# A two-block transformer on one core: first norm by a power operation, row scales moved out of two later norms, and five smaller moves

## The chip, the cores and the metric

The kernel runs on one core of one Trainium2 chip. The metric is device time in microseconds (us), from runs of the whole program. The core has a matrix engine (TensorE, PE in the profile, with its weight loads as PEld), a vector engine (VectorE, DVE), an activation engine (ScalarE, ACT), a general engine (GpSimd, POOL) and a queue engine that starts transfers (SyncE, SP). Matrix products write to the eight banks of PSUM; the other data is in SBUF.

## The reference

512 tokens of width 1024 go through two blocks, all in float32.

```
# first block
h = rmsnorm(x, norm_mix);  p = h @ w_in
y_ret  = retention(q, k, v, g of p; rotary sines and cosines of the positions)
y_rwkv = rwkv7(shifted p)          # gated delta-rule scan over time, group norm, bonus, gate
x = x + concat(y_ret, y_rwkv) @ w_out
x = x + cross_attention(rmsnorm(x, norm_xattn), rmsnorm(mem, norm_mem))   # 4 heads of 256, 256 memory rows
x = x + square(relu(rmsnorm(x, norm_mlp) @ w_up)) @ w_down                # 4096 wide
x = rmsnorm(x, norm_final)
# second block
h = rmsnorm(x); z = h @ w_in_2     # attention with axial rope, gated MLP with spatial mixing, merge gates
x = rmsnorm(x + merge(...) @ w_out_2)
```

A norm is `y = x * rsqrt(mean(x*x) + 1e-6) * gain`: one factor for each row (token) and one for each column.

## The kernel before

Tokens lie in four blocks of 128 rows. Every large product is made of three passes: each operand is split into a high part (a cast to fp32r, on ACT) and a low part (the rest, by a subtraction), and `mm3` adds high x high, high x low and low x high. Weights come as 512 KB units over SP's queue into three buffers, are split on ACT (L291, `wh`) and on DVE or POOL (L292, `wl`), and are used in order.

All matrix instructions keep the order in which the code writes them (`Ordered`). That order comes from generators: `streams` (L614) advances the main chain of products by one step, of some four matmuls, and then each side chain whose delay (`yield n`: n steps) or flag (`yield "name"`) has come. The other engines and the queues are ordered by the planner of the tile framework (`schedule_with_timeline_sim`), from its own estimate of durations: it puts an instruction on its engine when, by that estimate, its inputs are there and the engine is free, also ahead of earlier code. Each engine then works strictly in the order that was planned. What is changed lies here:

- `first` (L438): the first norm. The gain row is loaded to all 128 partitions; ACT squares four blocks; DVE makes `rsqrt` (L349, eleven small instructions) for two blocks at a time; blocks 0 and 1 are scaled on DVE, 2 and 3 on POOL and ACT; `turn` transposes eight 128x128 pieces for each block on PE, and splits them. Then the first product, 48 matmuls of 256 columns, follows.
- `trig` (L640): the angles' range reduction on POOL, some 60 instructions, and at its end two Sin activations on ACT (L685). The tables are used in the keys of the retention, much later.
- `products`, `invert`, `solve` (from L1521): RWKV's chunks. `invert` inverts 32x32 triangles on POOL, row by row; then two copies on ACT (L1586), transfers to DRAM and back (L1587 to L1595), and after 33 steps `solve` on PE reads the result. It is done twice, for two halves of the heads.
- `final_rw` (L818): for each of four pairs of heads transposes, an ACT instruction with weight and bias (L830), a POOL addition of `bv` (L831), a product with the gate (L836) and a split.
- `ret` (L750): the retention; `finish` transposes nine steps after its group norm.
- `run` (L428): one set of PSUM pools for the mixer (`mm`, `tp`, `cs`, `ch`, two banks each), and after it another (`mm` four, `tp`, `ch` two).
- `x1` (L975): the product with w_out in two halves of columns (`quad`), added to x (`add_x`, L936); `add_half` squares and multiplies by the gain on POOL (L955); `norm_end` makes the row's factor from the sums by `norm_scale`, multiplies (L970), and eight steps later transposes and splits. Then `tile_half` takes the first three Q tiles on the first 256 tokens and then on the rest. The second norm, for the MLP, is made in the same way after the product with w_o.
- `head`, `softmax` (L1051 to L1056): cross attention's scores with the scale 1/16.
- `heads` in `second` (L1174): rope in the second block.

Of the kernel before, what the change touches and what calls it, by code (L numbers as in the profile page):

```python
# [16 lines left out]
P = 128  # L17
# [65 lines left out]
def pack(inputs):  # L83
# [93 lines left out]
    for name, key in (("w0", "rwkv_w0"), ("a0", "rwkv_a0"), ("k_k", "rwkv_k_k"), ("k_a", "rwkv_k_a"), ("r_k", "rwkv_r_k"),  # L177
# [15 lines left out]
        "pv": pv,  # L193
        "rows": np.ascontiguousarray(rows),
# [34 lines left out]
class Kern:  # L229
# [34 lines left out]
    def psum(self, tag, shape=(P, 512)):  # L264
        return self.ps.tile(list(shape), F32, tag=tag, bufs=self.banks[tag], name=self.nm(tag))
# [162 lines left out]
    def run(self):  # L428
        nc, A, tc = self.nc, self.A, self.tc
        self.banks = {"mm": 2, "tp": 2, "cs": 2, "ch": 2}  # L430
        with tc.tile_pool(name="mx", bufs=1) as self.mp, tc.tile_pool(name="px", bufs=1, space=bass.MemoryType.PSUM) as self.ps:
            self.mix()
        self.banks = {"mm": 4, "tp": 2, "ch": 2}
        self.nh = 4
        with tc.tile_pool(name="m2", bufs=1) as self.mp, tc.tile_pool(name="p2", bufs=1, space=bass.MemoryType.PSUM) as self.ps:
            self.streams(self.rest())

    def first(self):  # L438
# [12 lines left out]
        g = self.gain("norm_mix", 6)  # L451
# [9 lines left out]
        v = [self.small(2) for _ in range(2)]  # L461
        rs = {}
        junk = self.slab(10, [P, 1024])

        def square(b):
            SC.activation(junk, xb[b], AF.Square, accum_out=v[b // 2][:, b % 2:b % 2 + 1])

        def chain(i):
            V.tensor_scalar(v[i], v[i], 1.0 / D, 1e-6, op0=ALU.mult, op1=ALU.add)
            r = self.rsqrt(v[i], 2, V=V)  # L470
            rs[2 * i], rs[2 * i + 1] = r[:, 0:1], r[:, 1:2]

        def scale(b):
            for h in range(2):
                c = slice(h * 512, h * 512 + 512)
                if b < 2:
                    V.scalar_tensor_tensor(xg[b][:, c], xb[b][:, c], rs[b], g[:, c], op0=ALU.mult, op1=ALU.mult)
                else:
                    SC.activation(xg[b][:, c], xg[b][:, c], AF.Copy, scale=rs[b])

        turn = lambda b: self.transp(xg[b], b, hh, V, SC, ("tp", "ch")[b % 2])
        for b in range(NB):
            square(b)
        for b in (2, 3):
            G.tensor_tensor(xg[b], xb[b], g, op=ALU.mult)
        chain(0)
        scale(0)
        scale(1)
        chain(1)
        turn(0)  # L490
        self.pump(0, 0, SC, G)
        turn(1)
        scale(2)
        scale(3)
        turn(2)
        turn(3)
        h, l = self.spl.pop(0)
        self.u = 1
        ps = self.psum("mm")
        for off in (0, 256):  # L500
            for k in range(KT):
                ah, al = h1[k]
                self.mm3(ps[:, off:off + 256], (h[:, k * 128:k * 128 + 128], l[:, k * 128:k * 128 + 128]),
                         (ah[:, off:off + 256], al[:, off:off + 256]), k == 0, k == KT - 1)
        derived(V)
# [134 lines left out]
    def trig(self):  # L640
# [45 lines left out]
        return  # L686
        yield
# [62 lines left out]
    def ret(self):  # L750
# [21 lines left out]
        def finish(n, y):  # L772
# [3 lines left out]
            yield 9  # L776
# [41 lines left out]
    def final_rw(self, hf, sl, s):  # L818
# [3 lines left out]
        for j in range(2):  # L822
# [7 lines left out]
            SC.activation(t, tr.rearrange("p c t -> p (c t)"), AF.Identity, bias=self.pv("rw_b", p), scale=self.pv("rw_w", p))  # L830
            G.tensor_tensor(t, t, self.bv[:, p], op=ALU.add)  # L831
# [108 lines left out]
    def add_half(self, st, b, j, ps, scale=None):  # L940
# [8 lines left out]
        self.flags.discard(f"norm {b}")  # L949
        ss, st[b][1] = st[b][0], self.tmp((P, 1024), "t4", 2)  # L950
        for i in range(4):
# [3 lines left out]
            nc.gpsimd.tensor_tensor(st[b][1][:, c], x[:, c], st["g"][:, c], op=ALU.mult)  # L955

# [7 lines left out]
    def norm_end(self, st, b, dst, rs=None, wait=None):  # L964

        ss, xg = st[b]
# [733 lines left out]
```

## Time and profile before

| | us |
|---|---|
| median of 3 runs | 1317.17 (1317.08 to 1317.53) |
| profiled execution | 1317.52 |
| its span, first to last instruction | 1315.7 |
| PE busy | 1244.0 (95%), 6972 matmuls |
| PEld, DVE, ACT, POOL busy | 1036.2, 708.0, 507.0, 472.7 |
| mean granted TensorE clock, share of full | 0.981 |

Times of events are counted from the start of the span. An engine's busy time is the sum over its instructions; "idle before" with a releaser says what ended an engine's wait. [...]

### The profile page before, as it was taken

What the parts mean: (1) busy time and instruction counts of PE and PEld (TensorE: products, weight loads), DVE (VectorE), ACT (ScalarE), POOL (GpSimd) and SP (SyncE); (2) the same over time, 40 slices, a digit from 0 to 9 for tenths busy, and PEclk for the clock granted to TensorE, in tenths of its full rate; (3) what the DMA queues carried; (4) which work ended last, traced back from release to release, by engine and by line L of the source; (5) the groups of instructions that cost most, each with busy time, mean ns of one, the idle gap of its engine ahead of it and who ended that gap; (6) DMA issues with size and microseconds to landing.
All of it is one profiled execution on the core that took longest, in us unless ns stands there. A gap on an engine that the chain in (4) does not pass through costs nothing.

```text
span 1315.7 us, 18199 instructions
## 1 busy us (share of the span) xinstructions
PE 1244.0 (95%) x6972; PEld 1036.2 (79%) x6972; DVE 708.0 (54%) x1493; ACT 507.0 (39%) x899; POOL 472.7 (36%) x515
## 2 busy tenths in 40 slices
PE   4989798999898989989999999999999999999997
PEld 4767678887797888879888888888787878788886
DVE  5756524447585555464333433342779946655355
ACT  5434334323344335333423322332544535454232
POOL 4914463235310352265201111111314672222474
PEclk9989899989999989998999999999999999999999
DMA  5312324112235131323333333332423232112321
GB/s 184 93 52 84 80 66 102 62 33 65 81 125 195 49 102 59 97 59 113 101 97 96 96 96 96 96 108 78 120 98 96 67 110 65 51 62 64 112 80 65
DMA packets 52376, 117.05 MB, mean 89 GB/s; under 512 B 23073, under 2 KB 23713, under 8 KB 52289
## 3 DMA queue, kind: packets, MB, share of 16 engines
q1 hardware_dynamic: 52112, 115.82, 29.0%
q8 instruction: 55, 0.90, 0.3%
q14 instruction: 33, 0.26, 0.1%
q0 software_dynamic: 32, 0.00, 0.0%
q10 hardware_dynamic: 144, 0.07, 0.0%
HBM read 112.46 MB, written 3.41 MB: 88 GB/s over the span
## 4 chain that ended last, share of the span: by engine, by line
PE 61%; DVE 5%; ACT 2%; issue 1%; POOL 1%; DMA 0%; DVEq 0%; ACTq 0%; POOLq 0%
PE mm L220 54%; PE ch L220 3%; PE tp L220 3%; DVE sm L362 1%; DVE sm L358 1%; PE cs L220 1%; DVE s L871 1%; ACT t L1054 0%; DVE t L1056 0%; ACT wh L291 0%; DMA raw<-wst 0%; DVE sm L1051 0%; DVE t L1117 0%; DVE s L1333 0%; POOL wlx L292 0%
## 5 line engine op out<-in xcount | busy, mean ns | idle before, releaser
L220 PE MATMUL mm<-s,wh 128*128 128x512 f32 (+1 forms) x1424 | 419.4, 376 | 0.3 <-DVE s L871 0.2
L220 PE MATMUL mm<-wh,s 128*128 128x512 f32 (+1 forms) x1232 | 351.0, 361 | 2.4 <-DVE s L871 1.4
L220 PEld LDWEIGHTS mm<-s,wh 128*128 128x128 f32 x1424 | 259.0, 191 | 51.3 <-issue 7.4
L220 PE MATMUL mm<-s,wl 128*128 128x512 f32 (+1 forms) x704 | 263.8, 375 | 0.0
L291 ACT CAST wh<-raw 128x1024 fp32r<-128x1024 f32 x151 | 158.6, 1050 | 257.3 <-PE mm L220 228.4
L220 PEld LDWEIGHTS mm<-wh,s 128*128 128x128 f32 x1232 | 223.0, 191 | 38.4 <-DVE s L871 1.8
L220 PE MATMUL mm<-wl,s 128*128 128x512 f32 (+1 forms) x616 | 219.4, 356 | 1.8 <-POOL wl L292 1.8
L292 DVE TENSOR_TENSOR wl<-raw,wh 128x1024 fp32r<-128x1024 f32 x99 | 123.7, 1249 | 166.5 <-ACT wh L291 164.0
L292 POOL TENSOR_TENSOR wl<-raw,wh 128x1024 fp32r<-128x1024 f32 x52 | 125.5, 2416 | 133.3 <-ACT wh L291 122.1
L220 PEld LDWEIGHTS mm<-s,wl 128*128 128x128 f32 x704 | 134.2, 191 | 21.1
L220 PEld LDWEIGHTS mm<-wl,s 128*128 128x128 f32 x616 | 117.5, 191 | 18.2 <-POOL wl L292 2.2
L1072 POOL TENSOR_TENSOR t<-t 128x512 f32<-128x512 f32 x32 | 49.9, 1560 | 215.0 <-ACT t L1071 215.0
L220 PE MATMUL mm<-s,whx 128*128 128x512 f32 (+1 forms) x336 | 101.3, 382 | 0.0
L220 PE MATMUL mm<-whx,s 128*128 128x512 f32 (+1 forms) x272 | 86.6, 378 | 0.9 <-DVE s L871 0.9
L220 PEld LDWEIGHTS mm<-s,whx 128*128 128x128 f32 x336 | 63.2, 197 | 10.6 <-DVE s L871 0.4
L347 DVE TENSOR_TENSOR s<-t,s 128x512 fp32r<-128x512 f32 x44 | 34.8, 791 | 65.4 <-ACT s L346 65.4
L220 PE MATMUL ch<-s,s 128*64 128x64 f32 (+3 forms) x504 | 62.7, 274 | 4.9 <-ACT s L1639 2.4
L292 POOL TENSOR_TENSOR wlx<-raw,whx 128x1024 fp32r<-128x1024 f32 x17 | 41.3, 2428 | 72.2 <-ACT whx L291 69.1
L220 PE MATMUL mm<-s,wlx 128*128 128x512 f32 (+1 forms) x168 | 63.8, 380 | 0.0
L291 ACT CAST whx<-raw 128x1024 fp32r<-128x1024 f32 x35 | 36.7, 1050 | 66.4 <-PE mm L220 50.6
L220 PEld LDWEIGHTS ch<-s,s 128*64 128x64 f32 (+2 forms) x504 | 46.5, 155 | 17.1 <-DVE s L871 3.7
L955 POOL TENSOR_TENSOR t<-s,s 128x256 f32<-128x256 f32 x48 | 34.2, 739 | 70.9 <-DVE s L936 57.6
(271 smaller groups left out, 1697.7 us busy)
## 6 DMA issues: line engine op xcount, KB each, us to landing
raw<-wst SPq DMA_DIRECT2D x189, 512.0 KB, 3.6
s<-x SPq DMA_DIRECT2D x8, 512.0 KB, 5.2
s<-rows SPq DMA_DIRECT2D x7, 512.0 KB, 4.2
out<-t SPq DMA_DIRECT2D x8, 256.0 KB, 2.3
t<-mem SPq DMA_DIRECT2D x2, 512.0 KB, 3.8
dm<-s SPq DMA_DIRECT2D x10, 64.0 KB, 2.0
s<-dm SPq DMA_DIRECT2D x2, 256.0 KB, 4.1
s<-dm SPq DMA_DIRECT2D x8, 64.0 KB, 2.4
```

The source lines that it names most:

```text
L220: r = getattr(self.eng, name)(*a, **k)
L291: (SC or nc.scalar).copy(h, r)
L292: (E or (nc.gpsimd if self.lowpart(self.nspl) else nc.vector)).tensor_tensor(l, r, h.bitcast(F32), op=ALU.subtract)
L347: self.nc.vector.tensor_tensor(dst[1], src, dst[0].bitcast(F32), op=ALU.subtract)
L358: V.scalar_tensor_tensor(t, y, h, y, op0=ALU.mult, op1=ALU.mult)
L362: V.scalar_tensor_tensor(y, t, 1.5, y, op0=ALU.add, op1=ALU.mult)
L871: (V or self.nc.vector).tensor_tensor(dst[1], ps, dst[0].bitcast(F32), op=ALU.subtract)
L955: nc.gpsimd.tensor_tensor(st[b][1][:, c], x[:, c], st["g"][:, c], op=ALU.mult)
L1072: nc.gpsimd.tensor_tensor(q, r, r, op=ALU.mult)
```

## The change

1. `first`: the gain is loaded as one row on ACT's queue and spread over 128 partitions by two products with a row of ones, into two PSUM banks. For each block DVE does one small instruction and POOL one power operation (exponent -0.5) on 128x1; all four blocks are scaled on DVE from PSUM. The first weight unit's low part is made on DVE in place of POOL. The first half of the first product starts on four of its eight k-tiles before block 3 is transposed.
2. `trig`: the two sines are written 95 steps later in the code.
3. `invert`: both copies on POOL in place of ACT.
4. `final_rw`: one DVE instruction in place of ACT's and POOL's; the bias is added to `bv` earlier, on POOL, in `recept`.
5. `ret`: 11 steps in place of 9; `heads`: three steps ahead of rope's last two POOL instructions, then 15 in place of 18.
6. One set of PSUM banks; in the second part `mm` tiles take turns, in pairs, between the banks `mm` and `cs`.
7. `x1`, `mlp`: the two norms are split up. `turn_half` transposes x itself, a half of the columns at a time; the gain, now one value for each partition (`gcol`), is applied in the splits (four ACT and four DVE instructions of 128x128 for a half block). The row factors of all four blocks are made together at the end. For cross attention they go into the softmax's scale, for the MLP, whose activation is a square, their square is applied where the down product is added to x.

```diff
     def psum(self, tag, shape=(P, 512)):
-        return self.ps.tile(list(shape), F32, tag=tag, bufs=self.banks[tag], name=self.nm(tag))
+        if tag == "mm" and self.nh == 4:
+            self.nmm += 1
+            tag = ("mm", "cs")[self.nmm // 2 % 2]
+        return self.ps.tile(list(shape), F32, tag=tag, bufs=2, name=self.nm(tag))
...
-        g = self.gain("norm_mix", 6)
+        gr = self.slab(6, [P, 1152])[0:1]
+        o, w = ROW["norm_mix"]
+        nc.scalar.dma_start(gr[:, 0:1024], A["rows"][0:1, o:o + w])
+        nc.gpsimd.memset(gr[:, 1024:1152], 1.0)
+        g = [self.psum("cs") for _ in range(2)]
+        for h in range(2):
+            self.T.matmul(g[h], gr[:, 1024:1152], gr[:, h * 512:h * 512 + 512], start=True, stop=True)
...
-        def chain(i):
-            V.tensor_scalar(v[i], v[i], 1.0 / D, 1e-6, op0=ALU.mult, op1=ALU.add)
-            r = self.rsqrt(v[i], 2, V=V)
+        def rms(b):
+            V.tensor_scalar(v[:, b:b + 1], v[:, b:b + 1], 1.0 / D, 1e-6, op0=ALU.mult, op1=ALU.add)
+            G.tensor_tensor(rs[:, b:b + 1], v[:, b:b + 1], mh[:, b:b + 1], op=ALU.pow)
...
+        square(0)
+        square(1)
+        square(2)
+        rms(0)
+        rms(1)
+        scale(0)
+        scale(1)
+        rms(2)
+        turn(0)
+        square(3)
+        scale(2)
+        rms(3)
+        turn(1)
+        self.pump(0, 0, SC, V)
+        scale(3)
+        turn(2)
+        product(0, range(4))
+        turn(3)
+        product(0, range(4, 8))
+        product(256, range(8))
...
-            V.tensor_scalar(x, x, -0.4999999, 0.4999999, op0=ALU.max, op1=ALU.min)
-            nc.scalar.activation(o, x, AF.Sin, scale=2.0 * math.pi)
+            V.tensor_scalar(o, x, -0.4999999, 0.4999999, op0=ALU.max, op1=ALU.min)
+        yield 95
+        for o in (self.sin, self.cos):
+            nc.scalar.activation(o, o, AF.Sin, scale=2.0 * math.pi)
...
-            SC.activation(t, tr.rearrange("p c t -> p (c t)"), AF.Identity, bias=self.pv("rw_b", p), scale=self.pv("rw_w", p))
-            G.tensor_tensor(t, t, self.bv[:, p], op=ALU.add)
+            V.scalar_tensor_tensor(t, tr.rearrange("p c t -> p (c t)"), self.pv("rw_w", p), self.bv[:, p], op0=ALU.mult, op1=ALU.add)
...
+    def turn_half(self, st, b, j, ps, dst, delay):
+        self.add_x(b, j, ps)
...
+            for k in range(4):
+                self.T.transpose(tr[:, k], x[:, k * 128:k * 128 + 128], self.ident)
+            for k in range(4):
+                g = st["g"][:, 4 * j + k:4 * j + k + 1]
+                nc.scalar.activation(h[:, k, c], tr[:, k], AF.Copy, scale=g)
+                nc.vector.scalar_tensor_tensor(l[:, k, c], tr[:, k], g, h[:, k, c].bitcast(F32), op0=ALU.mult, op1=ALU.subtract)
+            nc.scalar.activation(self.tmp(), x, AF.Square, accum_out=st["ss"][:, 2 * b + j:2 * b + j + 1])
...
+            if b == NB - 1:
+                yield 5
+                v = self.small(4)
+                nc.vector.tensor_reduce(v, st["ss"].rearrange("p (b j) -> p b j", j=2), axis=AX.X, op=ALU.add)
+                nc.vector.tensor_scalar(v, v, 1.0 / D, 1e-6, op0=ALU.mult, op1=ALU.add)
+                st["scale"](self.rsqrt(v, 4))
...
-            yield from self.quad(lambda k: y1[k], lambda b, ps: self.add_half(st, b, 0, ps))
-            yield from self.quad(lambda k: y1[k], lambda b, ps: self.x1_post(st, b, ps, hh), outer=True)
+            yield from self.quad(lambda k: y1[k], lambda b, ps: self.turn_half(st, b, 0, ps, hh, 3 + b))
+            yield from self.quad(lambda k: y1[k], lambda b, ps: self.turn_half(st, b, 1, ps, hh, 3), outer=True)
...
-            p = self.softmax(sc, 256, 1.0 / 16)
+            p = self.softmax(sc, 256, self.sq[:, b:b + 1], self.sq[:, b + 4:b + 5])
...
-                    yield from self.quad(lambda k: us[8 * g + k], lambda b, ps: self.add_x(b, j, ps))
+                    yield from self.quad(lambda k: us[8 * g + k], lambda b, ps: self.add_x(b, j, ps, self.sm2[:, b:b + 1]))
...
-            SC.copy(m[o, :, 0:16], w[o].rearrange("p i t -> p t i"))
+            G.tensor_copy(m[o, :, 0:16], w[o].rearrange("p i t -> p t i"))
```

## Rows read from the trace of the kernel before

**Rows 1.** PE's waits by releaser: us in total, times, longest us.
```profile
PE tp L220 <- DVE s L220: 14.2, 2, 12.6
PE tp L220 <- DVE t L970: 8.4, 2, 4.2
PE cs L220 <- DVE s L1538: 7.6, 1, 7.6
PE tp L220 <- ACT t L1446: 4.1, 1, 4.1
PE cs L220 <- DVE t L836: 3.1, 1, 3.1
PE tp L220 <- POOL t L1685: 2.9, 1, 2.9
PE mm L220 <- DVE s L871: 2.5, 3, 1.4
```

**Rows 2.** Stretches: us, busy PE, PEld, DVE, ACT, POOL (instructions), granted clock, DMA share, GB/s.
```profile
76.60:83.50 6.90, 6.90 (x19) 4.75 (x18) 4.49 (x8) 2.83 (x5) 0.19 (x1) 0.51 0.02 8
154.50:158.60 4.10, 4.10 (x20) 3.49 (x21) 4.10 (x7) 1.35 (x2) 0.00 (x0) 0.51 0.72 112
349.50:353.10 3.60, 3.59 (x22) 3.37 (x23) 1.98 (x3) 0.98 (x2) 0.25 (x1) 0.53 0.18 73
467.60:472.60 5.00, 4.98 (x24) 5.00 (x25) 4.12 (x10) 2.81 (x7) 3.79 (x3) 0.50 0.35 113
473.00:477.00 4.00, 4.00 (x36) 4.00 (x36) 2.30 (x7) 0.00 (x0) 0.00 (x0) 1.00 0.37 131
592.90:598.90 6.00, 6.00 (x29) 6.00 (x30) 5.09 (x14) 2.81 (x7) 3.79 (x3) 0.50 0.55 182
700.00:930.00 230.00, 229.96 (x1015) 190.24 (x1014) 81.49 (x110) 71.56 (x110) 35.53 (x26) 1.00 0.33 99
```

**Rows 3.** Order of time, the start: start us, us, engine line op out<-in xcount [idle before].
```profile
7.38 0.65 DVE L220 TENSOR_SCALAR sm<-sm 128x2 f32<-128x2 f32 x4 [7.38 <-ACT s L220]
24.21 1.29 DVE L220 TENSOR_TENSOR s<-tp,s 128x512 fp32r<-128x512 f32 x2 [0.76 <-ACT s L220]
31.15 0.63 PE L220 MATMUL mm<-s,wh 128*128 128x512 f32 x2
```

**Rows 4.** Groups by line and form: busy us, mean ns of one, idle before and releaser.
```profile
L1452 DVE SCALAR_TENSOR_TENSOR t<-kt,pv,tp 128x512 f32<-128x512 f32 x4 | 3.0, 748 | 7.4 <-PE tp L220 7.4
L292 DVE TENSOR_TENSOR wl<-raw,wh 128x1024 fp32r<-128x1024 f32 x99 | 123.7, 1249 | 166.5 <-ACT wh L291 164.0 <-PE mm L220 1.9
L1419 POOL COPY pc<-pt 128x8 f32<-128x8 f32 x4 | 1.0, 244 | 16.1 <-ACT pt L1418 16.1
L1072 POOL TENSOR_TENSOR t<-t 128x512 f32<-128x512 f32 x32 | 49.9, 1560 | 215.0 <-ACT t L1071 215.0
L220 POOL TENSOR_TENSOR s<-s,s 128x1024 f32<-128x1024 f32 x2 | 5.1, 2564 | 6.0 <-DMA s<-x 6.0
L782 ACT ACTIVATE t<-tp,pv 128x128 f32<-128x128 f32 x16 | 6.0, 457 | 6.6 <-PE tp L220 6.6
```

**Rows 5.** Order of time: the first sine on ACT, and a load on SP's queue.
```profile
71.13 0.31 ACT L685 ACTIVATE sin<-s 128x128 f32<-128x128 f32 x1 [7.02 <-POOL s L220]
...
528.34 0.33 SPq L376 DMA_DIRECT2D s<-rows  x1
```

**Rows 6.** Order of time, around the inverse.
```profile
149.98 2.14 ACT L1586 COPY s<-s 32x512 f32<-32x512 f32 x2 [9.64 <-POOL s L1581]
154.68 0.34 SPq L1591 DMA_DIRECT2D s<-dm  x1
163.83 0.84 PE L220 MATMUL cs<-s,s 32*32 32x32 f32 x21
```

**Rows 7.** The page's DMA issues: out<-in, queue, op, count, KB each, us to landing.
```profile
s<-dm SPq DMA_DIRECT2D x1, 128.0 KB, 2.5
```

**Rows 8.** Order of time: one instruction of the row factor's chain, on DVE.
```profile
458.48 2.38 DVE L362 SCALAR_TENSOR_TENSOR sm<-sm,sm 128x1 f32<-128x1 f32 x1
```

More of the change, by code (lines that the diff above doesn't have):

```diff
@@ L429, in run @@
         nc, A, tc = self.nc, self.A, self.tc
[L430 to L436, printed above, removed]
+        self.nmm = 0
+        with tc.tile_pool(name="px", bufs=1, space=bass.MemoryType.PSUM) as self.ps:
+            with tc.tile_pool(name="mx", bufs=1) as self.mp:
+                self.mix()
+            self.nh = 4
+            with tc.tile_pool(name="m2", bufs=1) as self.mp:
+                self.streams(self.rest())
     def first(self):
@@ L475, in scale, with product @@
                 c = slice(h * 512, h * 512 + 512)
[L476 to L479, printed above, removed]
+                V.scalar_tensor_tensor(xg[b][:, c], xb[b][:, c], rs[:, b:b + 1], g[h], op0=ALU.mult, op1=ALU.mult)
         turn = lambda b: self.transp(xg[b], b, hh, V, SC, ("tp", "ch")[b % 2])
[L482 to L501, printed above, removed]
+        def product(off, ks):
+            h, l = wa
+            for k in ks:
                 ah, al = h1[k]
@@ L955, in add_half, with turn @@
             nc.gpsimd.tensor_tensor(st[b][1][:, c], x[:, c], st["g"][:, c], op=ALU.mult)
+    def turn_half(self, st, b, j, ps, dst, delay):
+        nc = self.nc
+        self.add_x(b, j, ps)
+        if b + j == 0:
+            st["ss"] = self.small(8, "ss")
+        x = self.x[b][:, j * 512:j * 512 + 512]
+        if j:
+            self.flags.discard(f"norm {b}")
+        def turn():
+            h, l = dst[j]
+            c = slice(b * 128, b * 128 + 128)
+            tr = self.psum("tp", (P, 4, 128))
+            for k in range(4):
[5 more added lines that the diff above has]
+            nc.scalar.activation(self.tmp(), x, AF.Square, accum_out=st["ss"][:, 2 * b + j:2 * b + j + 1])
+            if j == 0:
+                return
+            self.flags.add(f"norm {b}")
+            if b == NB - 1:
+                yield 5
+                v = self.small(4)
+                nc.vector.tensor_reduce(v, st["ss"].rearrange("p (b j) -> p b j", j=2), axis=AX.X, op=ALU.add)
+                nc.vector.tensor_scalar(v, v, 1.0 / D, 1e-6, op0=ALU.mult, op1=ALU.add)
+                st["scale"](self.rsqrt(v, 4))
+        self.spawn(turn(), delay)
     def norm_scale(self, ss, scale=1.0 / D, eps=1e-6):
@@ L962, in norm_scale, with scale_q, scale_m @@
         return self.rsqrt(v, 1)
-    def norm_end(self, st, b, dst, rs=None, wait=None):
-        ss, xg = st[b]
-        rs = self.norm_scale(ss) if rs is None else rs
-        for h in range(2):
-            c = slice(h * 512, h * 512 + 512)
-            self.nc.vector.tensor_scalar(xg[:, c], xg[:, c], rs, None, op0=ALU.mult)
-        yield 8
-        self.transp(xg, b, dst)
-        self.flags.add(f"norm {b}")
-    def x1(self):
-        st = {"g": self.gain("norm_xattn", 4)}
+    def x1(self):
+        rows = self.mp.tile([P, 28], F32, name="rows")
+        g, self.sq, self.sm2 = rows[:, 0:16], rows[:, 16:24], rows[:, 24:28]
+        self.nc.sync.dma_start(g, self.A["gcol"])
+        V = self.nc.vector
+        def scale_q(rs):
+            V.tensor_scalar(self.sq[:, 0:4], rs, 1.0 / 16, None, op0=ALU.mult)
+            V.tensor_scalar(self.sq[:, 4:8], rs, -1.0 / 16, None, op0=ALU.mult)
+            self.flags.add("scale")
+        def scale_m(rs):
+            V.tensor_tensor(self.sm2, rs, rs, op=ALU.mult)
+        st = {"g": g[:, 0:8], "scale": scale_q}
         hh, hx = self.act4((7, 8, 5, 9))
@@ L1045, in head, with softmax @@
         self.flags.add(f"head {h}")
-    def softmax(self, sc, n, scale):
+    def softmax(self, sc, n, scale, minus=None):
         nc = self.nc
```

35 lines of the change are left out of this document (18 added, 17 removed).

## Prediction

> **What bounds the kernel now.** I read the page's busy times first: PE is busy 1244.0 of 1315.7 us, so at most 71.7 us are PE's waiting, and no change here takes a matmul of the large products away. Next PE's waits by releaser [rows 1]: seven kinds make up 42.8 us, and each belongs to a place that the change touches. Then the granted clock of the stretches behind the long waits [rows 2]: after five of them it stands at half, though PE has work. What that costs is read from two stretches with like work: 36 matmuls in 4.00 us at full clock (0.111 us each), 29 in 6.00 us and 24 in 5.00 us at half; at the full rate the 29 take 3.2 us and the 24 take 2.7, so 2.8 and 2.3 us are lost, 0.46 of such a stretch. A wait therefore costs its length and 0.46 of the slow stretch behind it.
>
> **The start.** The first transposes wait 12.6 us [rows 1], and the first product ends at 31.15, where the first 512-column matmuls stand [rows 3]. In the new order DVE carries the chain. It gets the second block's sum at 7.38 [rows 3] as before; one small instruction and a POOL power on 128x1 (0.24 us by the nearest small POOL row [rows 4]; block 0's was issued before) let scaling begin at 7.6. Then DVE does, for each of four blocks, two scalings from PSUM at 0.75 and two low parts at 0.645 [rows 3, 4], 11.1 us together, the first unit's low part 1.25 [rows 4], and some 0.2 of small ones: 20.2. The last half of the product, 24 matmuls at 0.111, would end at 22.9. PE must also fit block 3's transposes between two parts of the product, and ACT's casts lie ahead of each low part; I allow 2.2 us and take 25.1: a gain of 6.0. Ends: 8.2 with nothing lost, and 2.0 where a power takes as long as the largest POOL row, 2.56 [rows 4] (scaling 2.2 later), and the last part runs at half clock. The dropped 512 KB gain load frees SP's queue ahead of blocks 2 and 3; the new row is 4 KB on ACT's queue, and the two spreading products lie in time in which PE has nothing else. They cost nothing if the row has landed by about 6 us; each us later is a us on the path.
>
> **The sines.** ACT stood 7.0 us at the first Sin, waiting for POOL [rows 5], and the copy that PE needs was behind it: 4.1 us [rows 1], then 6.9 us at half clock [rows 2], 3.2 lost; 7.3 in all. The new place in the code binds only if the planner keeps it. It hoists by far more than that: the gain of the norm after the MLP, in the code after the eighth MLP tile (behind 592.9), was issued at 528.34, when its buffer came free [rows 5]. By the planner's estimate POOL is done early, which is why Sin stood there; ACT has free time in that stretch, so I expect the sines in nearly the same slots. I take 0; ends: 7.3 gained, 1.0 lost if both table changes fall ahead of the same copy.
>
> **The inverse's copies.** ACT stood 9.6 us at L1586 for POOL's last row [rows 6], behind it a gate activation, behind that DVE and PE: 7.6 us [rows 1] and then 4.1 us at half clock [rows 2], 1.9 lost. On POOL the copies follow their input in order, and ACT no longer waits: 9.5 gone. What is late next is the inverse itself. `solve` stood at 163.83 without a wait [rows 6]; 9.5 us sooner it is there at 154.3. Its data comes by a read issued at 154.68, which lands 2.5 later [rows 7], after two copies of 1.07 each [rows 6]. POOL's time for a copy of 512 elements is not in the trace: from 0.24 (the 128x8 copy) to 2.56 (128x1024, two inputs), nearest 1.56 (128x512) [rows 4], which I take. The data lands at 154.68 + 2 x 0.49 + 2.5 = 158.2, and PE waits 3.9 there. Net gain 5.6; ends 3.6 and 8.3 by the two other rows. Queued behind the copies on POOL are only the next half's fills, and `solve` for half two comes over 60 us later.
>
> [...]
>
> **RWKV's end.** PE waited 3.1 us for L836 and then had 3.6 us at half clock [rows 1, 2]: 4.8 at most. One DVE instruction (0.75 [rows 4]) replaces an ACT and a POOL instruction in series, but DVE also makes weight parts there, and the temporary buffer can be the real limit. I take 2.0; ends 0 and 4.8. The four additions of the bias lie on POOL early, behind nothing that PE reads soon.
>
> **Retention's end and the banks.** Two steps are eight matmuls, at 0.227 each (1015 in 230.0 us [rows 2]) 1.8 us, out of the 2.9 us wait on POOL L1685 [rows 1]. The 1.4 us wait on L871 [rows 1] is the first product of the next pool waiting for the last bank of the old one; with one set the first tile takes a bank long free. Together 3.2; ends 1.0 and 4.3. Otherwise two pairs of two banks turn like four: 0. The move in `heads`: 0; ends 0 and 1.8, if a weight part comes ahead of rope on POOL.
>
> **The two norms.** Both times PE waited 4.2 us for L970 [rows 1], with 5.0 and 6.0 us at half clock behind [rows 2]: 4.2 + 2.3 + 4.2 + 2.8 = 13.5. The wait was the chain of row factors on DVE, where an instruction of 128x1 took 2.38 [rows 8]. Now nothing small stands between x and its transposes: the second half of block 3 is needed by the second half of the Q tiles, 72 matmuls x 0.111 = 8.0 us after the product's end, and asks for two additions, four transposes and four casts, some 5 us with three steps of delay. The row factors are first read in the softmax, tens of us later. ACT pays: four activations of 0.46 [rows 4] for each half block in place of one cast, and the next units' casts stand in the same queue. I leave 1.5 for that: 12.0; ends 9 and 13.5. The squared factor in the MLP rides on an addition that is there anyway: 0. Gone as well are 32 POOL multiplications and two 512 KB loads.
>
> **Sum.** 6.0 + 0 + 5.6 + 2.0 + 3.2 + 12.0 = 28.8 us. Against the profiled execution, 1317.5, that is 1288.7; this execution lies 0.35 above the median, so 1288.4.
>
> **Rivals.**
> *The sines do move.* For: they are now the last of all instructions written for those 95 steps, so anything else ready on ACT goes first. Against: the hoisted load [rows 5]. Price 7.3: 1281.1. Chance 0.30.
> *The power is slow.* All four stand in the start's chain. If the first ends 6 us after its input, the gain of the start is gone: 1294.4. Against: POOL's small instructions take 0.24 [rows 4]. Chance 0.07. [...]
> *Transposes wait for ACT.* Sixteen half-block turns use two banks, each freed after four ACT and four DVE instructions, 1.8 us of ACT and a square; four turns come in a burst after each first half product. If each burst holds PE for 4 us, 8 us go: 1296.4. Chance 0.06.
> *Slower than before.* The same mechanism: each of the 16 half turns would have to hold PE for more than 28.8 / 16 = 1.8 us, a full turn of ACT's work with nothing beside it. A block's product takes 24 matmuls x 0.227 = 5.4 us and ACT needs about 2.7 plus a cast, so only a queue order that puts squares and casts first would do it: 1320. Chance 0.03.
> The forecast holds 0.54.
>
> **Numbers.** What a measurement of this kernel can tell from no change is about 0.2%, 2.6 us. The forecast's own ends reach from about 1283 to 1294; the sines pull the low end to 1277, slow powers and held banks the high end to 1298. Faster 0.95, same 0.02, slower 0.03.
>
> **What would show it.** After: the first 512-column matmul near 25; no wait on L970, its two slow stretches gone; ACT's copy of L1586 gone, PE past the gate tile without a wait, and a new wait of some 4 us at the first 32x32 matmuls; a Sin on ACT that still waits for POOL, with a PE wait of about 4 us behind it. The forecast is wrong if the sines stand 40 us later, if a power takes over 1 us, or if transposes of x wait for a bank.

## The result and the profile after

The changed kernel takes 1293.26 us (1293.14 to 1293.35, four runs), the kernel before 1317.12 beside it: ratio 0.9827, 95% interval 0.9812 to 0.9841 (the two medians alone give 0.9819, inside it). By the medians 23.9 us are gained where the prediction had 28.8. The profiled execution has a span of 1291.5 us; PE is busy as long as before and waits 47.9 us in place of 71.7.

The page's busy times:

```profile
PE 1243.6 (96%) x6976; PEld 1027.9 (80%) x6976; DVE 690.8 (53%) x1455; ACT 511.2 (40%) x921; POOL 455.5 (35%) x490
```

PE's waits by releaser in the changed kernel, a choice of rows (us in total, times, longest us), to be held against [rows 1]:

```profile
PE cs L221 <- DMA s<-dm: 9.4, 1, 9.4
PE cs L221 <- DMA s<-rows: 5.1, 1, 5.1
PE tp L221 <- DVE t L1165: 2.5, 1, 2.5
PE mm L221 <- POOL wl L296: 2.5, 1, 2.5
PE mm L221 <- DVE t L542: 2.0, 1, 2.0
PE tp L221 <- DVE s L992: 1.3, 2, 0.8
PE tp L221 <- POOL t L1736: 0.4, 1, 0.4
```

The two waits of 4.2 on the norms, the gate's 7.6, RWKV's 3.1 and the bank's 1.4 are gone. Where the norms' were, 1.3 us are left on L992, which makes the low part of x; the wait behind the sines is 2.0 (L542) in place of 4.1; the 5.1 us lie at the very start, where PE's first work is now the spreading of the gain row; and 9.4 us at the first 32x32 matmuls are new.

The stretches at half clock (us, busy PE, PEld, DVE, ACT, POOL, granted clock, DMA share, GB/s), beside [rows 2]:

```profile
75.30:78.70 3.40, 3.40 (x20) 2.43 (x20) 2.90 (x5) 0.61 (x1) 0.11 (x1) 0.50 0.64 171
147.00:160.60 13.60, 7.99 (x86) 6.72 (x87) 0.00 (x0) 1.20 (x2) 0.65 (x3) 0.50 0.75 166
932.00:935.40 3.40, 3.36 (x12) 2.80 (x11) 3.10 (x20) 1.17 (x2) 0.00 (x0) 0.51 0.00 0
```

Half clock stands behind the sines for 3.4 us (6.9 before) and no longer behind the norms; it stands around the new wait for 13.6. The third row lies in the second block, behind the 2.5 us wait on L1165, where the kernel before waited 2.1 us and kept the full clock.

How long half clock stands is not the same in every execution. Two further traces (experiment 6, first and third run) have the same instructions in the same order as the changed kernel, and there it stands for 20.4 us (149.6 to 170.0) and 20.6 (147.6 to 168.2) around the solve in place of 13.6, and PE falls back by another 3.2 to 3.3 us in that place. So from one trace a part's value is known only to some 3 us wherever half clock enters it.

How far the changed kernel is ahead can be read along the way, by the start of the same PE work in both traces (the same place in PE's order, by the count of matmuls on weights):

```
                                       before    after   ahead   this part   predicted
first products                          36.71    28.00     8.7     +8.7        6.0
transposes behind the sines            105.56    93.57    12.0     +3.3        0
end of the solve                       169.00   161.15     7.9     -4.2        5.6
end of the first chain of states       284.36   275.45     8.9     +1.1        -
behind RWKV's end                      355.27   340.88    14.4     +5.5        2.0
first product of the second pool       416.63   398.62    18.0     +3.6        3.2
inside the MLP                         633.29   603.88    29.4    +11.4       12.0
end                                   1315.7   1291.5     24.2     -5.2        0
```

That the lead in the MLP, 29.4, is near the forecast 28.8 is chance: four gains came larger, and the inverse lost. After that, 5.2 us go that no step of the prediction had.

### The profile page after: what moved, and what is told of

It reads as the page before. It is cut to its first block, busy times and chain, and to the rows that moved or that the text cites. A ratio compares the mean times of both kernels' runs of the same rounds, so it can differ in the third digit from the quotient of the medians.

```text
span 1291.5 us, 18137 instructions
## 1 busy us (share of the span) xinstructions
PE 1243.6 (96%) x6976; PEld 1027.9 (80%) x6976; DVE 690.8 (53%) x1455; ACT 511.2 (40%) x921; POOL 455.5 (35%) x490
## 4 chain that ended last, share of the span: by engine, by line
PE 79%; POOL 7%; DVE 6%; ACT 4%; issue 2%; DMA 2%; SPq 0%; ACTq 0%; DVEq 0%; POOLq 0%
PE mm L221 36%; PE cs L221 32%; PE ch L221 7%; PE tp L221 4%; POOL s L221 3%; POOL o L1630 1%; POOL s L1632 1%; ACT wh L295 1%; DVE wl L296 1%; DMA raw<-wst 1%; DMA s<-dm 1%; DVE s L887 1%; ACT t L1102 0%; DVE t L1104 0%; DMA dm<-s 0%
## 5 line engine op out<-in xcount | busy, mean ns | idle before, releaser
L221 PE MATMUL mm<-s,wh 128*128 128x512 f32 (+1 forms) x880 | 263.3, 379 | 2.2 <-DVE t L542 2.0
L221 PE MATMUL mm<-wh,s 128*128 128x512 f32 (+1 forms) x824 | 229.2, 347 | 1.2 <-DVE t L719 0.8
L296 DVE TENSOR_TENSOR wl<-raw,wh 128x1024 fp32r<-128x1024 f32 x99 | 123.2, 1244 | 171.3 <-ACT wh L295 170.8
L221 PEld LDWEIGHTS mm<-s,wh 128*128 128x128 f32 x880 | 159.0, 190 | 37.5 <-issue 7.2
L296 POOL TENSOR_TENSOR wl<-raw,wh 128x1024 fp32r<-128x1024 f32 x52 | 125.7, 2420 | 134.5 <-ACT wh L295 123.2
L221 PE MATMUL mm<-s,wl 128*128 128x512 f32 (+1 forms) x432 | 163.1, 378 | 1.0 <-DVE wl L221 1.0
L221 PE MATMUL cs<-s,wh 128*128 128x512 f32 (+1 forms) x544 | 154.2, 366 | 0.0
L221 PE MATMUL cs<-wh,s 128*128 128x512 f32 (+1 forms) x440 | 143.0, 389 | 0.0
L221 PEld LDWEIGHTS cs<-s,wh 128*128 128x128 f32 x544 | 97.8, 189 | 16.2 <-issue 0.2
L221 PE MATMUL cs<-s,wl 128*128 128x512 f32 (+1 forms) x272 | 99.7, 366 | 0.0
L221 PEld LDWEIGHTS cs<-wh,s 128*128 128x128 f32 x440 | 82.5, 190 | 16.4
L296 POOL TENSOR_TENSOR wlx<-raw,whx 128x1024 fp32r<-128x1024 f32 x17 | 41.3, 2428 | 136.4 <-ACT whx L295 133.2
L221 PE MATMUL cs<-wl,s 128*128 128x512 f32 (+1 forms) x220 | 85.5, 389 | 0.0
```

Source lines behind the costliest of these rows:

```text
L221: r = getattr(self.eng, name)(*a, **k)
L296: (E or (nc.gpsimd if self.lowpart(self.nspl) else nc.vector)).tensor_tensor(l, r, h.bitcast(F32), op=ALU.subtract)
```

## The experiments

Each run is timed beside the kernel before on its own chip; against the changed kernel it is compared by the two ratios, which leaves some 3 us of doubt, so smaller differences are read from traces. Line numbers below are those of the changed kernel.

**1. The inverse's copies back on ACT.**

```
-            G.tensor_copy(m[o, :, 0:16], w[o].rearrange("p i t -> p t i"))
+            SC.copy(m[o, :, 0:16], w[o].rearrange("p i t -> p t i"))
```

> The changed kernel with one thing undone: the inverse's two copies are on ACT again. My theory: moving the copies to POOL lost some 4 us where the prediction had a gain of 5.6, because with them on POOL the second of the two writes and the read that the solve needs stand late in SP's queue, behind the read-backs (read issued at 149.73, PE waits 9.4, half clock from 147.0 to 160.6). With the copies on ACT both writes leave together, the read is issued near 146 to 147, PE's wait at the first 32x32 matmuls falls from 9.4 to under 3 us, ACT stands some 8 to 10 us for POOL again and PE waits some 7 us ahead of it: in sum 2 to 5 us less than the changed kernel, 1288.5 to 1291.5. Rival: the 9.4 us come from POOL itself, which reaches the end of the inverse late against PE (new bias additions in its queue), and the side of the copies is worth what the prediction said: then the time rises by some 5 us, to 1298.

Measured: 1291.59 us, ratio 0.9815 (0.9796 to 0.9834). Order of time around SP's queue in the changed kernel (start us, us, line, out<-in; then PE):

```profile
141.91 2.24 POOL L1637 COPY s<-s 32x512 f32<-32x512 f32 x2
...
141.88 1.29 SPq L1640 DMA_DIRECT2D dm<-s  x2
143.26 0.64 SPq L1638 DMA_DIRECT2D dm<-s  x1
145.72 1.39 SPq L1646 DMA_DIRECT2D s<-dm  x3
147.21 0.59 SPq L1638 DMA_DIRECT2D dm<-s  x1
147.84 0.66 SPq L1646 DMA_DIRECT2D s<-dm  x1
148.54 1.03 SPq L1595 DMA_DIRECT2D dm<-s  x2
149.73 0.38 SPq L1642 DMA_DIRECT2D s<-dm  x1
...
152.61 0.60 PE L221 MATMUL cs<-s,s 32*32 32x32 f32 x8 [9.39 <-DMA s<-dm]
```

The same with the copies on ACT:

```profile
141.76 1.50 SPq L1638 DMA_DIRECT2D dm<-s  x2
144.27 0.87 SPq L1646 DMA_DIRECT2D s<-dm  x2
145.82 0.30 SPq L1642 DMA_DIRECT2D s<-dm  x1
...
146.74 0.58 PE L221 MATMUL cs<-s,s 64*128 64x128 f32 x1 [8.48 <-DVE s L1589]
```

With the copies on POOL the second write (L1638) stands behind three read-backs (L1646) that wait 1.7 us for the other data to land, and the read that the solve needs (L1642) comes last: 149.73 in place of 145.82. The order of events is as the theory has it, and the wait at the solve is gone. But the old wait is back at 8.5, and the time falls by only 1.6 us, just short of the theory's 2 to 5 and on the other side of the rival's. In the changed kernel the move of the copies is worth nothing, or a small loss.

**2. The same part alone, in the kernel before.**

```
-            SC.copy(m[o, :, 0:16], w[o].rearrange("p i t -> p t i"))
+            G.tensor_copy(m[o, :, 0:16], w[o].rearrange("p i t -> p t i"))
```

> The kernel before, with one part of the change alone: the inverse's two copies on POOL. The prediction gave this part 5.6 us: ratio 0.9957, with a wait of 3.9 us at the first 32x32 matmuls. My theory now: the planner, which counts a copy on POOL dearer than on ACT, splits the two writes and puts the read behind the read-backs in SP's queue, so the data lands some 9 to 10 us after POOL's last row in place of 7.2; PE's 7.6 us ahead of the gate go, and it waits 6 to 7 us at the first 32x32 matmuls in their place, with half clock behind as before. Gain 0 to 3 us: ratio 0.998 to 1.000. Rival: the wait at the solve in the changed kernel is due to POOL being late by the other additions alone; then the data is there within 4 us and the prediction's 5.6 us stand.

Measured: 1313.98 us, ratio 0.9979 (0.9967 to 0.9992), 2.8 us gained. Order of time around SP's queue in this run:

```profile
149.77 1.30 SPq L1589 DMA_DIRECT2D dm<-s  x2
...
154.04 0.58 SPq L1587 DMA_DIRECT2D dm<-s  x1
154.68 1.72 SPq L1595 DMA_DIRECT2D s<-dm  x3
156.63 0.30 SPq L1591 DMA_DIRECT2D s<-dm  x1
...
159.66 0.33 PE L220 MATMUL cs<-s,s 32*32 32x32 f32 x3 [6.80 <-DMA dm<-s]
```

The wait is 6.8, not 3.9, with half clock from 156.3 to 166.6 around it. PE gets the data 9.9 us after POOL's last row, which the first write (149.77) follows; the prediction had 8.2 from there (150.0 by [rows 6]) to 158.2. So the queue's order makes the data 1.5 us later than forecast. The half clock, for which the prediction has no term behind this wait, costs more: PE works 7.0 us in that stretch, and 0.46 of them are 3.2.

Nor does the trace show the 2.8 us at this part. Held against the kernel before at the same PE work, it is 2.0 us ahead at 145 already: 2.6 us come at the sines, which lie ahead of the edit (half clock for 3.4 us there in place of 6.8, and this wait in place of 4.1):

```profile
PE tp L220 <- ACT t L1446: 2.9, 1, 2.9
```

At the end of the solve it is 1.2 ahead. Across the inverse this trace loses 0.8 us, where the prediction had a gain of 5.6; what the measured 2.8 come from is open.

**3. The additions of the bias.** All four on DVE, and then all but the first:

```
-        self.nc.gpsimd.tensor_scalar(self.bv[:, p], self.bv[:, p], self.pv("rw_b", p), ...)
+        V.tensor_scalar(...)                                     # first run
+        (self.nc.gpsimd if p == 0 else V).tensor_scalar(...)     # second run
```

> The changed kernel with the four new additions of the bias, 128x512, on DVE in place of POOL (1.57 to 2.56 us each there). My theory: one of them lies inside the inverse's chain on POOL (114.75, 2.56 us) and one inside the sines' polynomial (60.56, 1.57 us). Without them POOL ends the inverse 2.5 us sooner, and the second write and the read for the solve stand sooner in SP's queue, so PE's wait at the first 32x32 matmuls falls from 9.4 to 3.5 to 5. But the planner then holds the sines for ready sooner and puts the first Sin ahead of the copy that PE needs, as in the kernel before: PE waits some 4 us there in place of 2.0, with 6.9 us at half clock. In sum 1 to 4 us less than the changed kernel. Rival: the additions lie in gaps of POOL's chain, and the inverse ends when PE's products let it: the wait at the solve stays over 8 us, and the time rises by the sines' 3 us.

> As the run with the bias on DVE, but the first of the four additions stays on POOL, so that the first Sin stays behind the copy that PE needs. My theory: the two effects come apart: PE waits 2.0 us at the sines as in the changed kernel, and 3.5 to 5 us in place of 9.4 at the first 32x32 matmuls, with a third to a half of the 13.6 us at half clock gone: 5 to 8 us less than the changed kernel, and 3 to 4 less than with all four on DVE. Rival: POOL's additions don't reach the solve: within 1.5 us of the changed kernel.

Measured: 1296.75 us, ratio 0.9869 (0.9844 to 0.9894), for all four; 1291.31, ratio 0.9815 (0.9799 to 0.983), for three. In the changed kernel one addition stands inside the inverse's chain on POOL:

```profile
114.35 0.42 POOL L1632 TENSOR_TENSOR s<-s,o 128x126 f32<-128x126 f32 x1
114.75 2.56 POOL L1541 TENSOR_SCALAR s<-s,pv 128x512 f32<-128x512 f32 x1
```

Without it POOL ends the inverse 2.1 us sooner and the solve starts 3.1 us sooner; with three on DVE, in order of time on PE, and then the row of a stretch:

```profile
149.52 0.39 PE L221 MATMUL cs<-s,s 32*32 32x32 f32 x4 [6.36 <-DMA dm<-s]
```

```profile
267.00:277.20 10.20, 10.20 (x62) 9.25 (x60) 2.75 (x15) 1.10 (x3) 4.43 (x7) 0.50 0.16 51
```

So the additions do reach the solve, but 6.4 us of wait are left where 3.5 to 5 were expected, and by 275 the lead is gone: 10.2 us at half clock stand there against 3.4 (269.9 to 273.3) in the changed kernel. The expected 5 to 8 us did not come: by the ratios it is 1.6. This trace is of the slowest of four executions (1289.5 to 1294.3 us), so whether that stretch is the edit's doing is not shown.

With all four on DVE the first Sin stands ahead of PE's copy. First that run in order of time on ACT, with PE's row, then ACT in the changed kernel:

```profile
60.02 1.28 ACT L704 ACT_TABLE_LOAD   x1
65.49 0.31 ACT L704 ACTIVATE sin<-sin 128x128 f32<-128x128 f32 x1 [4.19 <-POOL sin L221]
...
69.33 0.56 ACT L1495 COPY t<-ch 2x512 f32<-2x512 f32 x1
...
69.94 1.21 PE L221 MATMUL tp<-t,cst 2*128 2x512 f32 x1 [6.60 <-ACT t L1495]
```

```profile
60.72 0.58 ACT L1495 COPY t<-ch 2x512 f32<-2x512 f32 x1
61.31 1.28 ACT L704 ACT_TABLE_LOAD   x1
66.26 0.31 ACT L704 ACTIVATE sin<-sin 128x128 f32<-128x128 f32 x1 [3.66 <-POOL sin L221]
```

The two runs differ in one POOL addition of 1.57 us, and it decides whether PE's copy (L1495) waits out the sines; that it does so through the planner's estimate is argued, not read. The direction was as expected, the size not (6.6 us of wait, not 4, and 10.4 us at half clock, 67.6 to 78.0, not 6.9), and so the sign of the sum was wrong: 5.5 us slower than the changed kernel where 1 to 4 less were expected.

**4. The sines at their old place in the code** (both in the loop, no `yield 95`).

```
-            V.tensor_scalar(o, x, -0.4999999, 0.4999999, op0=ALU.max, op1=ALU.min)
-        yield 95
-        for o in (self.sin, self.cos):
-            nc.scalar.activation(o, o, AF.Sin, scale=2.0 * math.pi)
+            V.tensor_scalar(x, x, -0.4999999, 0.4999999, op0=ALU.max, op1=ALU.min)
+            nc.scalar.activation(o, x, AF.Sin, scale=2.0 * math.pi)
```

> The changed kernel with the sines at their old place in the code (both in one loop, no 95 steps of delay). My theory: the new place in the code does nothing, since the planner hoists the sines anyway; that PE waits 2.0 us in place of 4.1 there, with 3.4 us at half clock in place of 6.9, comes of ACT's copy for PE (60.72) now being planned ahead of the first Sin, which it is as well with the old place. So the same time within 1.3 us, 1292 to 1294.6, and Sin behind the copy. Rival: the new place is what put the copy first; then Sin stands ahead of it again and the time rises by 3 to 4 us, to 1297.

Measured: 1298.83 us, ratio 0.9868 (0.9849 to 0.9886). That is 5.4 us slower than the changed kernel, and the theory fell. So did the rival, for Sin is behind the copy as the theory said; but the cosine stands one instruction sooner, with one more change of tables ahead of PE's next copies. ACT and PE in this run:

```profile
71.22 0.31 ACT L702 ACTIVATE cos<-s 128x128 f32<-128x128 f32 x1
71.53 1.28 ACT L1469 ACT_TABLE_LOAD   x1
...
77.59 0.79 PE L221 MATMUL mm<-s,wh 128*128 128x512 f32 x1 [3.35 <-DVE t L542]
```

PE waits 3.35 in place of 1.96 and then has 6.9 us at half clock in place of 3.4; 3.6 us are lost by 102. Of these, 1.4 were lost at the start already, where half clock stands from 15.8 to 19.2; the changed kernel's trace has none there, the first run of experiment 6 has it with the same instructions (16.4 to 19.8). So the cosine's place is worth some 2.2 us in this trace. Another 2.7 are lost between 206 and 217, where half clock stood longer; why is open.

**5. The start without power operations:** the old chain of nine small DVE instructions for each block.

```
-            G.tensor_tensor(rs[:, b:b + 1], v[:, b:b + 1], mh[:, b:b + 1], op=ALU.pow)
+            rs[b] = self.rsqrt(v[:, b:b + 1], 1, V=V)
```

> The changed kernel with the four power operations on POOL replaced by the old chain of small instructions on DVE (nine of 0.2 us for each block); the order of the start and the spread weights stay. My theory: DVE carries the start, and the power operations (0.56 us each on POOL, beside DVE's work) are worth what they take off DVE: some 1.8 us for each of blocks 1 to 3 and less for block 0, whose scaling waits for the spread weights until 8.9 as it is. The first 512-column matmul comes at 27 to 29 in place of 22.4, and the time rises by 4.5 to 6.5 us against the changed kernel. Rival: the gain of the start is that of the order and of the weights spread by PE, and DVE has enough gaps: the 512-column matmul at 23 to 25, and under 2.5 us lost.

Measured: 1302.3 us, ratio 0.9892 (0.9878 to 0.9907). In order of time, the first power operation and the first 512-column matmul of the changed kernel, then that matmul in this run:

```profile
6.10 0.57 POOL L221 TENSOR_TENSOR sm<-sm,sm 128x1 f32<-128x1 f32 x1 [2.29 <-DVE sm L221]
...
22.44 0.63 PE L221 MATMUL mm<-s,wh 128*128 128x512 f32 x2
```

```profile
29.59 0.63 PE L221 MATMUL mm<-s,wh 128*128 128x512 f32 x2
```

The matmul comes 7.2 us later, and the run is 8.6 us slower than the changed kernel; expected were 27 to 29 and 4.5 to 6.5. Of the 7.2, 5.3 are DVE's: its low part of the third block starts at 22.40 in place of 17.14. The rest comes with half clock from 18.6 to 25.4, where the changed kernel's trace has none. So DVE carries the start, as theory and prediction had it, and with the rest of the new start in place the power operations are worth 5 to 7 us of the 8.7.

What else the change takes away there was not tried alone. In the kernel before, DVE's first two scalings take 5.54 us (from 9.76) while POOL multiplies two blocks (9.66 to 14.76), and the two after that only 1.33. In the changed kernel POOL does no such work, and a scaling takes 0.69 to 0.75.

**6. The address of the weight buffers.** In the changed kernel a tile of 112 bytes stands ahead of the second pool, and its four big buffers lie 128 bytes higher. Three runs: that tile behind them; a dead tile of that size in the kernel before; the tile 256 bytes wide.

```
+        for t in ("whx", "wlx"):                          # first run: the buffers first
+            self.mp.tile([P, 1024], F32R, tag=t, ...)     # (and s16, s17)
         rows = self.mp.tile([P, 28], F32, name="rows")
+        self.mp.tile([P, 28], F32, name="pad")            # second run, in the kernel before
-        rows = self.mp.tile([P, 28], F32, name="rows")    # third run
+        rows = self.mp.tile([P, 64], F32, name="rows")
```

> The changed kernel, with only the place of a 112-byte tile in SBUF changed: the new tile of norm gains and row factors lies behind the fourth weight buffers (whx, wlx) and the two slabs of the second pool in place of ahead of them, so these four lie at the addresses that they had before the change, 128 bytes lower. Every instruction and its order stay. My theory: matmuls that read these buffers start 232 to 233 ns apart in the changed kernel and 227 before, which makes 3.9 us for whx and wlx and some 1.4 us for the rest, and it is the address that does it: 1288 to 1290 (4 to 5 us less), with 226.7 ns between matmuls in the MLP. Rival: the slower matmuls come from the two pairs of PSUM banks that the changed kernel alternates between, or from other transfers beside them; then nothing changes, 1293.3.

> The kernel before, with one unused tile of 112 bytes put ahead of the second pool, so that the fourth weight buffers (whx, wlx) and the two slabs of that pool lie 128 bytes higher, where the changed kernel has them. No instruction and no order changes. My theory: the address alone makes matmuls that read these buffers start 232 ns apart in place of 227; about 1060 matmuls by the kernel's code read whx and wlx or stand between those that do, which made 5 us in the changed kernel: the ratio to the kernel before is 1.003 to 1.0045, 4 to 6 us slower. Rival: the slow matmuls need the changed kernel's two pairs of PSUM banks as well; then the ratio is 0.999 to 1.001 and all matmuls of the MLP start 227 ns apart.

> The changed kernel with its new tile 256 bytes wide in place of 112, so that the weight buffers of the second pool lie 256 bytes above their places before, in place of 128. Theory: what counts is where a buffer lies modulo 256 bytes beside the other operands (all others lie at 192, the shifted ones at 64, and with this run at 192 again): 227 ns between matmuls on whx and wlx and 1288 to 1290. Rival: any place but the old one is slower (a boundary of 2048 bytes falls 64 bytes into the old buffers, and lies outside the first 512 elements of the shifted ones): 230 ns or more, and 1292 to 1294.

Measured: 1288.48 us, ratio 0.9787 (0.9769 to 0.9805); for the kernel before with the dead tile 1321.97, ratio 1.0045 (1.003 to 1.006); with 256 bytes 1288.76, ratio 0.9788 (0.9772 to 0.9804). Sixty microseconds of the MLP at full clock (columns as above; the number of matmuls stands behind PE's time), in the changed kernel, the kernel before with the dead tile, and the one with 256 bytes:

```profile
652.00:712.00 60.00, 60.00 (x264) 49.29 (x264) 23.47 (x33) 17.63 (x22) 8.21 (x6) 1.00 0.32 97
```

```profile
680.00:740.00 60.00, 60.00 (x264) 49.30 (x264) 22.49 (x33) 17.65 (x22) 8.19 (x6) 1.00 0.32 97
```

```profile
652.00:712.00 60.00, 60.00 (x267) 49.69 (x266) 23.58 (x32) 17.55 (x22) 7.95 (x5) 1.00 0.32 97
```

The kernel before has 266 there. In all three traces the clock is full and PE never idle. The 3 matmuls are lost at whx and wlx: 668 that read them, one behind the other, start 232.6 ns apart on the mean in the changed kernel, 227.4 with the buffers back or at 256. All three runs fell as the theory said. It is the address, not the banks of PSUM: the kernel before, with its old banks, slows by the dead tile alone.

**7. The solve ten steps later** (`self.wait = [43, 25]` for `[33, 25]`).

> The changed kernel with one number changed: the solve of the first half comes 43 in place of 33 steps after its products in PE's order, so about ten pieces of other products (some 0.9 us each) lie ahead of it. My theory: PE's wait of 9.4 us at the first 32x32 matmuls is a matter of order alone, since the data lands at 152.5 whatever PE does; the wait falls under 1.5 us and most of the 13.6 us at half clock go with it: 9 + 3 = 12 us less than the changed kernel, 1281 to 1284. Rival: the chain of states that follows the solve is what decides, and main work moved ahead of the solve is missed later as cover for the chain's waits: then a gain of under 4 us, 1289 to 1294.

Measured: 1288.45 us, ratio 0.9779 (0.9755 to 0.9802): 6.3 us less than the changed kernel, between the two theories. PE's row, and two stretches:

```profile
152.08 0.28 PE L221 MATMUL cs<-s,s 32*32 32x32 f32 x4 [1.37 <-DMA s<-dm]
```

```profile
153.00:166.70 13.70, 13.70 (x127) 11.11 (x125) 1.82 (x2) 4.00 (x6) 5.97 (x16) 0.50 0.58 174
221.30:231.50 10.20, 9.75 (x103) 9.26 (x102) 5.35 (x13) 4.83 (x10) 0.00 (x0) 0.50 0.31 102
```

The wait was order alone and can be covered, as the theory said. That the half clock would go with it was wrong: it stands for 13.7 us, from 0.9 us after the small matmuls began, although PE worked at full clock until 1.4 us ahead of them. The second stretch lies in the chain of states, where the changed kernel has 3.4 us at half clock (205.0 to 208.4); the rival's cost is there too. The five executions lie between 1282.7 and 1290.2 us, and this trace is of the second fastest.

**8. RWKV's end undone:** ACT scales, POOL adds, as before.

```
-            V.scalar_tensor_tensor(t, tr..., self.pv("rw_w", p), self.bv[:, p], op0=ALU.mult, op1=ALU.add)
+            SC.activation(t, tr..., AF.Copy, scale=self.pv("rw_w", p))
+            G.tensor_tensor(t, t, self.bv[:, p], op=ALU.add)
```

> The changed kernel with RWKV's end as before: scale on ACT, then the addition on POOL, in place of one instruction on DVE (the bias stays added beforehand). My theory: the chain of one ACT and one POOL instruction is what PE waited 3.1 us for, and the half clock behind it cost 1.6: 3.5 to 5 us slower than the changed kernel, 1296.5 to 1298.5, with a PE wait of 2.5 to 3.5 us near 336. Rival: the earlier end of the other streams has taken that wait's place already, and the edit is worth under 1.5 us.

Measured: 1299.48 us, ratio 0.9871 (0.9846 to 0.9895), 5.8 us slower, with the wait where it was expected:

```profile
337.38 0.58 PE L221 MATMUL cs<-s,s 64*128 64x128 f32 x2 [3.05 <-DVE t L853]
```

Between 277 and 341 this trace falls back by 6.8 us against the changed kernel's, half of it at half clock (337.1 to 343.9). That reading is what the verdict rests on: the six executions lie between 1293.9 and 1304.8 us, and the one in the trace (1294.3) makes up most of the loss in other places, where less half clock stands (its mean granted clock is 0.99, the changed kernel's 0.988).

**9. Three things mended together:** the tile behind the buffers, three additions on DVE, `self.wait = [40, 25]`.

> The changed kernel with three of the studied things together: the 112-byte tile behind the weight buffers, three of the four bias additions on DVE, and the first half's solve 40 in place of 33 steps after its products. My theory: the three add up but for their overlap, 4.8 us by the addresses and 5 to 8 by the wait at the solve, which is covered by other products now: PE waits under 2 us at the first 32x32 matmuls and 227 ns lie between matmuls in the MLP: 1280 to 1284, ratio 0.973 to 0.976. Rival: what the solve gains is given back in the chain of states behind it, through PE's waits and the clock there; then only the addresses count, 1287 to 1289.

Measured: 1281.7 us, ratio 0.9736 (0.9718 to 0.9754), inside the expected range: 12 us faster than the changed kernel, 35 faster than before.

```profile
150.46 0.31 PE L221 MATMUL cs<-s,s 32*32 32x32 f32 x5 [1.05 <-DMA dm<-s]
177.88 0.55 PE L221 MATMUL ch<-st,s 128*128 128x128 f32 x1 [5.34 <-DVE st L1710]
```

The solve waits 1.05 us. A new wait of 5.3 in the chain of states, with half clock from 175.0 to 185.2, takes part of it back, as the rival said it might.

## Why the prediction came out as it did

- **Start** (6.0; measured 8.7). The step was right: DVE ended its low parts at 19.8 where 20.2 were worked out. The 2.2 us allowed for casts and transposes were not needed. Half clock did not enter this trace; in two others with the new start (experiments 4 and 6) it did, and the first 512-column matmul came 1.4 and 1.7 us later, so the gain is 7.0 to 8.7. That the spreading products cost nothing if the row lands by 6 us was nearly so: it landed at 5.1, and DVE still waited 0.7 for the second product. The slow power did not come: the first took 0.57 us and began 0.1 us after its input was ready, the others took 0.55 to 0.56. No run shows the 6 us from input to end that this rival is priced by.
- **Sines** (0; measured 3.3). The slot was foreseen, and Sin does wait for POOL, 3.7 us in the changed kernel. What failed is "nearly the same slots" as a price of nothing: one place among ACT's instructions is worth 2 us of PE's time by the place of the cosine (experiment 4) and 6 by the place of the copy that PE needs (experiment 3). No 4 us wait stood behind Sin any more, as it should have by the prediction's signs.
- **Inverse** (5.6; measured a loss of 4.2). This is the step that failed. The wait that goes was right (9.5 with its half clock). The new one is 9.4, not 3.9, with 8.0 us of work at half clock behind it, 3.7 lost: 9.5 - 13.1 = -3.6, beside -4.2 read. The prediction priced the new wait by its length alone, although by its own rule the slow stretch behind a wait costs as well; that term is 3.7 us here and 3.2 when the copies move alone (experiment 2). Against a lead of 12.0 us the data should have landed at 158.2 - 12.0 = 146.2; PE got it at 152.6. Of these 6.4 us, 3.9 are POOL's: its last row ends just ahead of the write at 141.88, and 150.0 - 12.0 = 138.0 would have kept the lead; 2.56 of that is the addition "behind nothing that PE reads soon", which lay in the inverse's own chain (with three additions away POOL ended 2.1 us sooner, experiment 3). The other 2.5 are SP's queue: 10.7 us from that write to the solve, not 8.2. The copy itself was cheaper than taken, 1.12 us each and not 1.56.
- **RWKV's end** (2.0; measured 5.5, and 5.8 when undone, 6.8 in its trace, with some half clock each time). The value was undersized: the whole 4.8 came, and DVE's other work did not stand in the way.
- **Retention's end and the banks** (3.2; measured 3.6). Right, as far as the traces tell: the wait on the bank is gone, and 0.4 us are left of the 2.9 [rows 1]. No run undoes this part.
- **Norms** (12.0; measured 11.4). Right in place and kind, a little large: the 1.3 us left on L992 are transposes that wait for a bank until DVE has read it. That is the third rival's mechanism at a sixth of its price; transposes that wait for a bank were also one of the signs by which the forecast was to be wrong, and this one came true in small. No run tests the norms alone. Why a 128x1 instruction of the old chain took 2.38 us [rows 8] the prediction did not ask. POOL's row of that time:

```profile
458.43 2.41 POOL L292 TENSOR_TENSOR wlx<-raw,whx 128x1024 fp32r<-128x1024 f32 x1 [0.55 <-ACT whx L291]
```

It begins 0.05 us ahead of DVE's instruction and ends 0.02 ahead of its end. All twelve DVE instructions of one or two columns that took over 1.5 us in the kernel before, eight of them in the two norms, ended within 0.03 us of the end of a POOL instruction that was running as they began. In the changed kernel two of each norm's row factors still do (448.65 and 450.78, 128x4, 1.96 and 2.28 us), but nothing on PE waits for them then. That POOL holds DVE there is read from the times; no run tests it.
- **Second half** (0; measured a loss of 5.2). No step had it. The address explains it: 3.9 us at whx and wlx and 1.4 beside them by the spacing, 5.1 to 5.9 by the three runs, which also take in PE's wait on POOL L296 (2.5; 1.8 with the buffers back, as in the kernel before).

So the inverse came 9.8 us short, the second half 5.2 and the norms 0.6; start, sines, RWKV's end, retention and the chain of states (half clock there 6.8 us in place of 10.3) brought 11.0 beyond their terms, and the sum is 4.6 short. The time lies inside the range in part by luck: two errors of 10 and 5 us were nearly covered by gains that the terms did not have, some of them half clock that need not come out the same in the next execution.

## What to carry to other kernels

When a producer moves to another engine, follow what its new place does to the queue of the DMAs behind it, and to every other edit that puts work on that engine: here a 2.6 us addition, two writes split apart and the half clock behind the new wait turned an expected gain into a loss. Price a new wait as the old ones are priced, with the slow stretch behind it (3.7 us here). A new small tile ahead of big buffers is an edit of its own (112 bytes cost 5.1 to 5.9 us here by the three runs); compare the spacing of matmuls at full clock before looking for waits. A chain of small DVE instructions is worth taking out of PE's way where POOL works beside it: twelve such instructions took 1.8 to 2.4 us in the kernel before, most of the others 0.14 to 0.22. And where a wait depends on order alone, moving independent work ahead of it is the cheaper cure, though only a part of its length came back here (6.3 us of a wait of 9.4).

## What the runs showed of the hardware

- Matmuls of 128x512 (fp32r) that read buffers shifted by 128 bytes started 232.6 ns apart in place of 227.4, at full clock and without a wait; with a shift by 256 bytes it was 227.4 again. By the program's addresses the fast ones and the other operands of the large products lie at 192 modulo 256, the slow ones at 64. Which of the operands' distances does it, and why, stays open.
- The four power operations of 128x1 on POOL took 0.55 to 0.57 us.
- The four additions of a 128x1 scalar to 128x512 on POOL took from 1.57 to 2.56 us in the changed kernel.
- DVE instructions of one or two columns, mostly 0.14 to 0.22 us long, took 1.8 to 2.4 us twelve times in the kernel before, each until a POOL instruction of 128x1024 that was running at its start had ended.
- Half clock stood around the solve for 13.6, 20.4 and 20.6 us in three traces of the same instructions in the same order.
